# Linear attention: a head's decays, scores and states as three steps, tied behind the projections of a written order

## The chip, the cores and the metric

The kernel runs on one core of a Trainium2 chip. The metric is the device time of one execution in microseconds (us); lower is better. The core has a matrix engine (TensorE; PE in the profile, and PEld for its weight loads), a vector engine (VectorE, DVE), an activation engine (ScalarE, ACT), GpSimd (POOL) and SyncE (SP), which here mainly issues DMA transfers. Each engine takes its own instructions in the order in which they were put in its queue.

## The reference, cut to what matters

A diffusion-style block (token mixer with a gated delta rule and gated linear attention, then a mixture of 32 experts) is followed by two layers of a second block. The change lies in the gated linear attention (GLA) of the mixer: 4 heads, key size 128, value size 256, 256 context tokens and 256 latent tokens, each head scanned forwards and backwards.

```python
def gla_chunked(q, k, v, log_a, s0):          # S_t = diag(a_t) S_{t-1} + k_t v_t^T, o_t = S_t^T q_t
    gcum = jnp.cumsum(log_a, axis=-2)          # the decays, summed along a chunk
    ref = gcum[..., c // 2:c // 2 + 1, :]
    attn = einsum('bhnik,bhnjk->bhnij', q * exp(gcum - ref), k * exp(ref - gcum))   # scores
    intra = einsum('bhnij,bhnjv->bhniv', where(incl, attn, 0.0), v)
    qg, kd, gl = q * exp(gcum), k * exp(gcum[..., -1:, :] - gcum), exp(gcum[..., -1, :])
    def step(s, xs_n):
        o_n = intra_n + einsum('bhck,bhkv->bhcv', qg_n, s)
        s = s * gl_n[..., :, None] + einsum('bhck,bhcv->bhkv', kd_n, v_n)           # states
```

Around it stand the input projections (1024 inputs, more than 9000 columns), SiLU and sigmoid gates of them, an RMS norm of each head's output, and the output projections.

## The kernel before, in words

Everything here is in `phase1`, which ends before the experts begin. The projections are matrix products in a split precision: `load_w` (L172) brings 512 KB of weights from HBM through a ring of three buffers on SP's queue, `parts` splits them into a high part `wh` on ACT (L150) and a rest `wl` on DVE (L151), each in a pool of two buffers, and `mm3` (L164) makes three matmuls for each product, those with `wh` first and those with `wl` last. `proj_fm` uses one such load (24 matmuls of 256 columns for the latent tokens), `proj_tm` two loads (48 matmuls for two token tiles, 96 for four).

Tiles share buffers by tag. In PSUM there are two buffers of tag `mm` and two of `sm`, three of `ch` and one of `pu`. A planner in the framework (its scheduler) puts the instructions into the queues of the engines. It gets them in the order in which the program names them, keeps every dependence on data and buffers, and may put a later named instruction of an engine ahead of an earlier one if by its own model of times the earlier one would still be waiting.

The stage in question comes after the delta rule and is driven by the string `GLA_ORDER`, one letter for one piece of work:

- `D`, a head's gates, both directions. `gla_gates(h, d)` does one direction from end to end. First the decays: a small product into `ch` (L807, PE), the log-sigmoid `z`, `l` (L810 to L814, DVE and ACT), running sums `G` (L818, DVE), and from these on ACT and DVE the scaled queries and keys `qk` (L828 to L835), `off` (L837 to L841), `qs` (L842 to L844), `glt` (L846) and `kd` (L848 to L852). Then the scores: `kd` is transposed on PE (L855) and copied to `kdt` by ACT (L857); PE makes the scores (L862, L863), and DVE copies them under a mask into `AT` (L864). Then the states: PE (L868) into `pu`, ACT copies (L869), PE again (L871), DVE (L872) into `gs`. It returns `qs`, `AT` and `gs`.
- `O`, `outputs(h)`: the products of a head's `qs` with `gs` and of `AT` with the values `gv`, for both directions (L947, L948, PE), in buffers of tag `mm`.
- `v`: values of heads 2 and 3 (`proj_tm`, four tiles, all buffers of `mm` and `sm`); there are two `gv` buffers, so head 2's takes the place of head 0's.
- `S`: RMS of two delta heads, a quarter of the gate `z` (`silu_cols`, `proj_tm`), and `columns`, which multiplies, transposes on PE (L924) and splits (L929, L930). `R`: the same projection for the GLA branch. `B`: RMS and `columns` of one GLA head. `G` and `b`: one of eight sigmoid gates each (`gate_cols`, `proj_fm`).

The string before is `DSGGGGOvDSGODGSORvDSRGRBBBGbORbbBbbbbb`. Nothing in this stage but data, buffers and the planner's model sets where a piece stands in PE's queue. After the stage come the output projections (`w_out_a`, `w_out_b`), and on SP's queue the first weights of the experts.

Of the kernel before, what the change touches and what calls it, by code (L numbers as in the profile page):

```python
# [9 lines left out]
F32 = mybir.dt.float32  # L10
F32R = mybir.dt.float32r
# [176 lines left out]
DELTA_ORDER = "EkPPKPKPKPKMmXXXXXXXXXPQPQPVVHHkqSSSSSSSSPPQPQPVVHHSSSSSSSSEkPPKPKPKPKMXXXXXXXXXPQPQPVmVHHSSSSSSSSkPPQPQPVqqVHHSSSSSSSSqvv"  # L188


GLA_ORDER = "DSGGGGOvDSGODGSORvDSRGRBBBGbORbbBbbbbb"


def phase1(k, A, B):
# [25 lines left out]
    def smps(cols=512):  # L220
        return ps.tile([128, 512], F32, name=k.nm("sm"), tag="sm", bufs=2)[:, :cols]
# [8 lines left out]
    def big(shape, dt=F32):  # L230

        return y8.tile([128] + shape, dt, name=k.nm("y8"), tag="y8")
# [93 lines left out]
    for kk in range(8):  # L326
# [5 lines left out]
                                    op0=ALU.mult, op1=ALU.add)  # L332
        nc.vector.tensor_sub(hTl[:, kk, :], hf, hTh[:, kk, :].bitcast(F32))

    def at(x, i):
        return x[i] if isinstance(x, Halves) else x[:, i, :]

    def proj_fm(src, xh, xl):

        wh, wl = parts(k, load_w(k, src))  # L340
        o = mmps(xh.shape[-1])
        mm3(nc, o, [(wh[:, kk, :], wl[:, kk, :], at(xh, kk), at(xl, kk), True) for kk in range(8)], True, True)
        return o

    def proj_tm(src, tiles, xh, xl, evac):

        os_ = [None] * len(tiles)
        for half in range(2):
            wh, wl = parts(k, load_w(k, src[512 * half:512 * half + 512, :]))
            for i, t in enumerate(tiles):  # L350
                if half == 0:
                    os_[i] = ps.tile([128, 256], F32, name=k.nm("tm"), tag=("mm", "sm")[i // 2], bufs=2)
                ts = slice(t * 128, (t + 1) * 128)
                mm3(nc, os_[i], [(wh[:, kk, :], wl[:, kk, :], at(xh, 4 * half + kk)[:, ts], at(xl, 4 * half + kk)[:, ts], False)
                                 for kk in range(4)], half == 0, half == 1)
        for i, t in enumerate(tiles):
            evac(t, os_[i])

# [443 lines left out]
    def gla_gates(h, d):  # L802

        f = d == 0
        kT, qT = gk[h], gq[h]
        pz = ps.tile([128, 512], F32, name=k.nm("ch"), tag="ch", bufs=3)
        nc.tensor.matmul(pz, gw[32 * d:32 * d + 16, h * 128:(h + 1) * 128], lr[32 * d:32 * d + 16, :], start=True, stop=True)  # L807
        T2 = lambda nm, tag, b=2: (wd if tag == "kt" else wk).tile([128, 512], F32, name=k.nm(nm), tag=tag, bufs=b)
        z, l = T2("z", "acc"), T2("l", "e", 3)
        nc.vector.tensor_scalar_add(z, pz, vecT[:, 24 + 4 * d + h:25 + 4 * d + h])  # L810
        nc.scalar.activation(l, z, AF.Abs)
        nc.scalar.activation(l, l, AF.Exp, scale=-1.0)
        nc.scalar.activation(l, l, AF.Ln, bias=1.0)
        nc.vector.scalar_tensor_tensor(z, z, 0.0, l, op0=ALU.min, op1=ALU.subtract)  # L814
        G = T2("G", "kt")
        for c0, c1 in ((0, 256), (256, 384), (384, 512)):
            st = 1 if f else -1
            nc.vector.tensor_tensor_scan(G[:, c0:c1][:, ::st], one1.to_broadcast([128, c1 - c0]), z[:, c0:c1][:, ::st],  # L818
                                         0.0, op0=ALU.mult, op1=ALU.add)
        g2 = G[:, 256:512].rearrange("p (t c) -> p t c", c=128)  # L820
        g4 = G[:, 256:512].rearrange("p (t c) -> p t c", c=64)
        fh, sh = (slice(0, 64), slice(64, 128)) if f else (slice(64, 128), slice(0, 64))
        bnd = g2[:, :, 63:64] if f else g2[:, :, 64:65]
        fi = 0 if f else 1
        tc_, tl = (G[:, 255:256], G[:, 383:384]) if f else (G[:, 0:1], G[:, 384:385])
        x = wd.tile([128, 256], F32, name=k.nm("x"), tag="qT", bufs=4)
        x4 = x.rearrange("p (t c) -> p t c", c=64)
        nc.vector.tensor_tensor(x4, g4, g4[:, :, (32 if f else 31):(33 if f else 32)].to_broadcast([128, 4, 64]),  # L828
                                op=ALU.subtract)
        qk = wd.tile([128, 512], F32, name=k.nm("qk"), tag="kT", bufs=5)  # L830
        qe, ke = qk[:, 0:256], qk[:, 256:512]
        nc.scalar.activation(qe, x, AF.Exp, scale=0.0625)
        nc.scalar.activation(ke, x, AF.Exp, scale=-0.0625)
        nc.vector.tensor_mul(qe, qe, qT)
        nc.vector.tensor_mul(ke, ke, kT[:, 256:512])  # L835
        off = wd.tile([128, 2, 2, 64], F32, name=k.nm("off"), tag="qT", bufs=4)
        nc.vector.tensor_tensor(off[:, 0], g2[:, :, sh], bnd.to_broadcast([128, 2, 64]), op=ALU.subtract)  # L837
        nc.vector.tensor_tensor(off[:, 1], bnd.to_broadcast([128, 2, 64]), g2[:, :, fh], op=ALU.subtract)
        nc.scalar.activation(off, off, AF.Exp, scale=0.0625)
        nc.vector.tensor_mul(off[:, 0], off[:, 0], qT.rearrange("p (t c) -> p t c", c=128)[:, :, sh])  # L840
        nc.vector.tensor_mul(off[:, 1], off[:, 1], kT[:, 256:512].rearrange("p (t c) -> p t c", c=128)[:, :, fh])  # L841
        qs = wd.tile([128, 256], F32, name=k.nm("qs"), tag="os", bufs=2)  # L842
        nc.scalar.activation(qs, G[:, 256:512], AF.Exp, scale=0.0625)
        nc.vector.tensor_mul(qs, qs, qT)  # L844
        glt = wd.tile([128, 1], F32, name=k.nm("glt"), tag="glt", bufs=2)
        nc.scalar.activation(glt, tl, AF.Exp, scale=0.0625)  # L846
        kd = wd.tile([128, 384], F32, name=k.nm("kd"), tag="pad", bufs=2)
        nc.vector.tensor_tensor(kd[:, 0:256], tc_.to_broadcast([128, 256]), G[:, 0:256], op=ALU.subtract)  # L848
        nc.vector.tensor_tensor(kd[:, 256:384], tl.to_broadcast([128, 128]), g2[:, fi, :], op=ALU.subtract)
        nc.scalar.activation(kd, kd, AF.Exp, scale=0.0625)  # L850
        nc.vector.tensor_mul(kd[:, 0:256], kd[:, 0:256], kT[:, 0:256])
        nc.vector.tensor_mul(kd[:, 256:384], kd[:, 256:384], kT[:, 256 + fi * 128:384 + fi * 128])  # L852
        pk = smps(384)
        for t in range(3):
            nc.tensor.transpose(pk[:, t * 128:(t + 1) * 128], kd[:, t * 128:(t + 1) * 128], ident)  # L855
        kdt = wd.tile([128, 3, 128], F32, name=k.nm("kdt"), tag="A2", bufs=2)
        nc.scalar.copy(kdt.rearrange("p t c -> p (t c)"), pk)  # L857
        AT = wd.tile([128, 2, 128], F32, name=k.nm("AT"), tag="st", bufs=2)
        nc.gpsimd.memset(AT, 0.0)
        for t in range(2):  # L860
            pa = chps()
            nc.tensor.matmul(pa, ke[:, t * 128:(t + 1) * 128], qe[:, t * 128:(t + 1) * 128], start=True, stop=True)  # L862
            nc.tensor.matmul(pa[fh, sh], off[:, 1, t, :], off[:, 0, t, :], start=True, stop=True)  # L863
            nc.vector.copy_predicated(AT[:, t, :], m_gla[:, 128 * d:128 * d + 128], pa)  # L864
        ss_ = wd.tile([128, 2, 256], F32, name=k.nm("gs"), tag="vb", bufs=2)
        p0 = ps.tile([128, 256], F32, name=k.nm("pu"), tag="pu", bufs=1)
        for t in range(2):
            nc.tensor.matmul(p0, kdt[:, t, :], gv[h][:, t, :], start=(t == 0), stop=(t == 1))  # L868
        nc.scalar.copy(ss_[:, 0, :], p0)  # L869
        p1 = ps.tile([128, 256], F32, name=k.nm("pu"), tag="pu", bufs=1)  # L870
        nc.tensor.matmul(p1, kdt[:, 2, :], gv[h][:, 2 + fi, :], start=True, stop=True)  # L871
        nc.vector.scalar_tensor_tensor(ss_[:, 1, :], ss_[:, 0, :], glt, p1, op0=ALU.mult, op1=ALU.add)  # L872
        return qs, AT, ss_

    def silu_cols(c0, dst, ccs=range(4)):

# [64 lines left out]
    def outputs(h):  # L941
        for t in range(2):
# [5 lines left out]
                nc.tensor.matmul(po, AT[:, t, :], gv[h][:, 2 + t, :], start=False, stop=(d == 1))  # L948
            nc.scalar.copy(ob[:, t, h, :], po)

    for c in GLA_ORDER:
        i = count.setdefault(c, 0)
        count[c] += 1
        if c == "D":
            two[i] = [gla_gates(i, d) for d in range(2)]
        elif c == "O":
            outputs(i)
        elif c == "S":
            ba_.rms(2 * i, 2)
            silu_cols(3072, z, (i,))  # L960
            ba_.columns(i)
        elif c == "G":
            gate_cols(7232, ga, (i,))
        elif c == "v":
            fill_gv(i + 2)
        elif c == "R":
            silu_cols(6176, rr2, (i,))
        elif c == "B":
            if not bb:
                bb = [Branch(ob, 4, rr2, 33, big([8, 256], F32R), big([8, 256], F32R))]  # L970
            bb[0].rms(i, 1)
            bb[0].columns(i)
        else:
            gate_cols(8256, gb_, (i,))
    bb = bb[0]
# [1127 lines left out]
```

## Time and profile before

| | us |
|---|---|
| three runs | 2461.91, 2469.0, 2471.72 |
| median | 2469.0 |
| the profiled execution, its own time | 2463.59 |
| its span, first to last instruction | 2461.8 |

In the page's busy time PE has 2277.9 us (93% of the span), PEld 1546.1 (63%), DVE 1244.0 (51%), ACT 925.4 (38%), POOL 150.9 (6%). The mean granted clock of TensorE is 0.969 of full speed. HBM was read at 245 GB/s over the span. The 40 slices of the page are 61.5 us each: the GLA stage runs from the end of slice 8 to the middle of slice 11, and the experts' weights stream in slices 14 to 27. Times of views count from the start of the span. A PE row's busy time overlaps its neighbours', since a matmul starts before the one ahead of it has drained.

### The profile page before, as it was taken

How to read it: one execution, taken by the hardware profiler on the slowest of the kernel's cores; microseconds unless marked ns; L12 is line 12 of the kernel's file. 1: busy time of each engine (PE TensorE's matmuls, PEld its weight loads, DVE VectorE, ACT ScalarE, POOL GpSimd, SP SyncE). 2: the span in 40 equal slices, each digit the busy share in tenths (PEclk: the TensorE clock that was granted, in tenths of full speed). 3: DMA queues.
4: the chain of work that ended last, by engine and by line, in shares of the span. 5: the costliest groups of instructions: out<-in, count | busy, mean ns of one | idle time of the engine just before them, and what ended most of it. 6: DMA issues, size and time to landing. Idle time of an engine off the chain costs nothing.

```text
span 2461.8 us, 36281 instructions
## 1 busy us (share of the span) xinstructions
PE 2277.9 (93%) x14402; PEld 1546.1 (63%) x14403; DVE 1244.0 (51%) x2676; ACT 925.4 (38%) x1956; POOL 150.9 (6%) x186
## 2 busy tenths in 40 slices
PE   6789878999989999999899999998999999999998
PEld 3466556889983433333334333334877999887998
DVE  4898887587561111112211111114867556867655
ACT  4556546577441101010101010103475545465545
POOL 0122122000010000000000000000011001011001
PEclk8889988999999999999999999999999999999999
DMA  8522431134897999999999999996525555534563
GB/s 288 141 79 57 121 116 35 47 92 122 260 333 307 419 420 419 420 419 420 391 419 419 421 418 420 419 420 232 149 79 156 183 172 159 155 98 141 188 188 104
DMA packets 273963, 605.87 MB, mean 246 GB/s; under 512 B 26038, under 2 KB 218681, under 8 KB 221564
## 3 DMA queue, kind: packets, MB, share of 16 engines
q1 hardware_dynamic: 266852, 595.24, 65.7%
q10 hardware_dynamic: 6280, 7.80, 1.2%
q8 instruction: 115, 1.88, 0.3%
q14 instruction: 60, 0.49, 0.1%
q0 software_dynamic: 656, 0.46, 0.1%
HBM read 602.30 MB, written 1.15 MB: 245 GB/s over the span
## 4 chain that ended last, share of the span: by engine, by line
PE 34%; DMA 10%; DVE 4%; issue 2%; ACT 1%; POOL 0%; ACTq 0%; SPq 0%; DVEq 0%; POOLq 0%
PE qm L164 23%; DMA w<-in_w_gu_dram 7%; PE yd L1376 2%; DMA w<-in_w_down_dram 2%; PE gt L1360 2%; PE lt L1360 1%; PE qm L1814 1%; DVE wl L151 1%; PE tr L1345 1%; DVE u L1620 0%; DVE ul L151 0%; PE tr L1289 0%; PE qp L1881 0%; ACT wh L150 0%; PE lt L1365 0%
## 5 line engine op out<-in xcount | busy, mean ns | idle before, releaser
L150 ACT CAST wh<-w 128x1024 fp32r<-128x1024 f32 (+2 forms) x318 | 318.5, 1002 | 285.4 <-PE qm L164 203.6
L151 DVE TENSOR_TENSOR wl<-w,wh 128x1024 fp32r<-128x1024 f32 (+2 forms) x318 | 371.4, 1169 | 39.9 <-ACT wh L150 38.2
L1253 ACT ACTIVATE sg<-g 128x1024 f32<-128x1024 f32 x16 | 16.9, 1057 | 720.4 <-DVE g L1251 720.4
L164 PE MATMUL qm<-uh,wh 128*128 128x272 f32 (+2 forms) x1008 | 261.8, 294 | 0.5 <-ACT wh L150 0.3
L164 PE MATMUL qm<-ul,wh 128*128 128x272 f32 (+2 forms) x1008 | 258.4, 289 | 1.2 <-DVE ul L151 1.2
L1251 DVE TENSOR_SCALAR g<-gt 128x1024 f32<-128x1024 f32 x16 | 19.6, 1225 | 462.9 <-PE gt L1365 407.3
L1376 PE MATMUL yd<-w,aT 128*64 128x512 f32 x1024 | 228.6, 601 | 0.0
L164 PEld LDWEIGHTS qm<-uh,wh 128*128 128x128 f32 (+1 forms) x1008 | 189.2, 188 | 10.2 <-issue 5.8
L164 PEld LDWEIGHTS qm<-ul,wh 128*128 128x128 f32 (+1 forms) x1008 | 189.9, 189 | 3.1 <-DVE ul L151 1.6
L1360 PE MATMUL lt<-w,resB 128*64 128x512 f32 x512 | 187.9, 593 | 0.6 <-DVE act L1252 0.6
L1360 PE MATMUL gt<-w,resB 128*64 128x512 f32 x512 | 183.0, 600 | 4.8 <-DMA w<-in_w_gu_dram 4.8
L1360 PE MATMUL lt<-w,xg 128*64 128x512 f32 x512 | 185.3, 593 | 0.0
L1360 PE MATMUL gt<-w,xg 128*64 128x512 f32 x512 | 175.3, 597 | 8.6 <-DMA w<-in_w_gu_dram 8.5
L1376 PEld LDWEIGHTS yd<-w,aT 128*64 128x64 f32 x1024 | 73.0, 139 | 142.6 <-issue 139.8
L1275 DVE TENSOR_TENSOR ys<-yd,g2r 128x512 f32<-128x512 f32 x32 | 20.6, 686 | 249.5 <-PE yd L1376 233.0
L164 PE MATMUL qm<-uh,wl 128*128 128x272 f32 (+2 forms) x1008 | 145.4, 286 | 0.0
L164 PE MATMUL mm<-hTh,wh 128*128 128x256 f32 (+1 forms) x384 | 130.1, 358 | 8.5 <-ACT wh L150 4.1
L164 PEld LDWEIGHTS qm<-uh,wl 128*128 128x128 f32 (+1 forms) x1008 | 132.6, 188 | 0.5 <-issue 0.4
L164 PE MATMUL qm<-fl,wh 128*128 128x272 f32 (+1 forms) x512 | 128.5, 286 | 0.0
L164 PE MATMUL qm<-fh,wh 128*128 128x272 f32 (+1 forms) x512 | 127.3, 286 | 0.0
L164 PE MATMUL mm<-hTl,wh 128*128 128x256 f32 (+1 forms) x384 | 125.9, 347 | 0.0
L1360 PEld LDWEIGHTS lt<-w,resB 128*64 128x64 f32 x512 | 57.7, 137 | 74.1 <-issue 72.1
(586 smaller groups left out, 4349.3 us busy)
## 6 DMA issues: line engine op xcount, KB each, us to landing
w<-in_w_gu_dram SPq DMA_DIRECT2D x256, 1024.0 KB
w<-in_w_down_dram SPq DMA_DIRECT2D x128, 1024.0 KB
w<-in_w_ff_dram SPq DMA_DIRECT2D x64, 1024.0 KB
w<-in_w_in_dram SPq DMA_DIRECT2D x72, 512.0 KB
w<-in_w_in_dram SPq DMA_DIRECT2D x30, 1024.0 KB
y<-in_w_mod_dram SPq DMA_DIRECT2D x19, 1024.0 KB
w<-in_w_out_dram SPq DMA_DIRECT2D x24, 512.0 KB
w<-in_w_mod_dram SPq DMA_DIRECT2D x5, 1024.0 KB
```

The lines of the kernel that those rows point to most:

```text
L150: k.nc.scalar.copy(hi, x)
L151: k.nc.vector.tensor_sub(lo, x, hi.bitcast(F32))
L164: mm = nc.tensor.matmul(out, l, r, start=start and n == 1, stop=stop and n == 3 * len(terms))
L1251: nc.vector.tensor_scalar(g, gt, 7.0, LOW / 1.702, op0=ALU.min, op1=ALU.max)
L1253: nc.scalar.activation(sg, g, AF.Exp, scale=-1.702)
L1275: nc.vector.tensor_mul(ys[:, js], yd[:, js], g2r[:, js])
L1345: nc.tensor.matmul(o, hx[:, t, f * 128:(f + 1) * 128], S[t].rearrange("p e s -> p (e s)"), start=(t == 0 and i == 0), stop=(t == 1 and i = ...
L1360: nc.tensor.matmul(quarter(j)[64 * i:64 * i + 64], xg[:, kk, c0:c0 + CAP], w[i][:, j * 512:(j + 1) * 512], start=(kk == 0), stop=False)
L1376: nc.tensor.matmul(yd[64 * i:64 * i + 64, j * 512:(j + 1) * 512], aT[:, 2 * f2 + f, 64 * i:64 * i + 64], w[i][:, f, j * 512:(j + 1) * 512] ...
L1814: nc.tensor.matmul(o[r, f:], v[:n, j, r], keys(ts[i], j, n)[:, f - KQ[j]:], start=(j == 0), stop=(j == 2))
```

## The change

The string becomes a longer one of 62 letters. `D` is gone: `gla_gates` is now a generator that stops twice, and each direction of each head is three letters, `d` (decays, up to `kd`), `e` (transposes and scores) and `f` (states). `S` is split too: `s` does the RMS and the projection, `C` does `columns`. The letters `d`, `e`, `f`, `O`, `C` and `B` run under `tc.issue_after(made_by[0].ins)`, where `made_by[0]` is the last matmul of the projection named last: every PE instruction of such a letter must stand behind that matmul in PE's queue. The instructions of other engines get no such edge, and a projection may still be put ahead. `qs` takes a buffer of tag `kT` (five of them) and no longer one of the two of tag `os`. No instruction is added or removed.

```diff
-GLA_ORDER = "DSGGGGOvDSGODGSORvDSRGRBBBGbORbbBbbbbb"
+
+GLA_ORDER = "dsdGCefdGGGGefOdvefdsGCefOdvefdsGCefOdRsefGCRBefORBBbRbbBbbbbb"
...
+    made_by = [None]
+
...
-        mm3(nc, o, [(wh[:, kk, :], wl[:, kk, :], at(xh, kk), at(xl, kk), True) for kk in range(8)], True, True)
+        made_by[0] = mm3(nc, o, [(wh[:, kk, :], wl[:, kk, :], at(xh, kk), at(xl, kk), True) for kk in range(8)], True, True)
...
-                mm3(nc, os_[i], [(wh[:, kk, :], wl[:, kk, :], at(xh, 4 * half + kk)[:, ts], at(xl, 4 * half + kk)[:, ts], False)
-                                 for kk in range(4)], half == 0, half == 1)
+                made_by[0] = mm3(nc, os_[i], [(wh[:, kk, :], wl[:, kk, :], at(xh, 4 * half + kk)[:, ts],
+                                               at(xl, 4 * half + kk)[:, ts], False) for kk in range(4)], half == 0, half == 1)
...
-        qs = wd.tile([128, 256], F32, name=k.nm("qs"), tag="os", bufs=2)
+        qs = wd.tile([128, 256], F32, name=k.nm("qs"), tag="kT", bufs=5)
...
         nc.vector.tensor_mul(kd[:, 256:384], kd[:, 256:384], kT[:, 256 + fi * 128:384 + fi * 128])
+        yield
         pk = smps(384)
...
             nc.vector.copy_predicated(AT[:, t, :], m_gla[:, 128 * d:128 * d + 128], pa)
+        yield
         ss_ = wd.tile([128, 2, 256], F32, name=k.nm("gs"), tag="vb", bufs=2)
...
-        return qs, AT, ss_
+        yield qs, AT, ss_
...
+    def pinned(c, i):
+        if c in "def":
+            h, d = divmod(i, 2)
+            if c == "d":
+                two.setdefault(h, []).append(gla_gates(h, d))
+                next(two[h][d])
+            else:
+                x = next(two[h][d])
+                if c == "f":
+                    two[h][d] = x
+        elif c == "O":
+            outputs(i)
+        elif c == "C":
+            ba_.columns(i)
+        else:
+            if not bb:
+                bb.append(Branch(ob, 4, rr2, 33, big([8, 256], F32R), big([8, 256], F32R)))
+            bb[0].rms(i, 1)
+            bb[0].columns(i)
+
     for c in GLA_ORDER:
         i = count.setdefault(c, 0)
         count[c] += 1
-        if c == "D":
-            two[i] = [gla_gates(i, d) for d in range(2)]
-        elif c == "O":
-            outputs(i)
-        elif c == "S":
+        if c in "defOCB":
+            with tc.issue_after(made_by[0].ins):
+                pinned(c, i)
+        elif c == "s":
             ba_.rms(2 * i, 2)
             silu_cols(3072, z, (i,))
-            ba_.columns(i)
...
-        elif c == "B":
-            if not bb:
-                bb = [Branch(ob, 4, rr2, 33, big([8, 256], F32R), big([8, 256], F32R))]
-            bb[0].rms(i, 1)
-            bb[0].columns(i)
```

With heads and directions written out, the new string begins d(0,0) s0 d(0,1) G0 C0 e(0,0) f(0,0) d(1,0) G1 G2 G3 G4 e(0,1) f(0,1) O0 d(1,1) v2 e(1,0) f(1,0) d(2,0) s1 G5 C1 e(1,1) f(1,1) O1 d(2,1) v3, and goes on e(2,0) f(2,0) d(3,0) s2 G6 C2 e(2,1) f(2,1) O2 d(3,1) R0 s3 e(3,0) f(3,0) G7 C3 R1 B0 e(3,1) f(3,1) O3 R2 B1 B2 b R3 b b B3 and five more b.

## Rows read from the trace of the kernel before

**Rows 1.** The page's 40 slices: busy tenths, granted clock, transfer rate.

```profile
PE   6789878999989999999899999998999999999998
...
PEclk8889988999999999999999999999999999999999
...
GB/s 288 141 79 57 121 116 35 47 92 122 260 333 307 419 420 419 420 419 420 391 419 419 421 418 420 419 420 232 149 79 156 183 172 159 155 98 141 188 188 104
```

**Rows 2.** Stretches: PE, PEld, DVE, ACT, POOL busy (instructions), clock, DMA share, GB/s.

```profile
474.00:641.90 167.90, 164.96 (x1205) 149.88 (x1204) 131.52 (x320) 120.99 (x300) 1.87 (x6) 1.00 0.43 119
641.90:650.00 8.10, 5.75 (x36) 5.55 (x35) 3.71 (x5) 5.64 (x10) 2.34 (x1) 0.79 0.69 205
```

**Rows 3.** Waits of PE's matmuls, 474.5 to 646: total us, times, longest.

```profile
PE ch L862 <- DVE qk L835: 2.8, 6, 0.6
PE mm L164 <- ACT wh L150: 2.4, 1, 2.4
```

**Rows 4.** Groups of PEld, 474.5 to 642: busy, mean ns | idle before, releasers.

```profile
L164 PEld LDWEIGHTS tm<-wh,hTh 128*128 128x128 f32 x189 | 35.7, 189 | 1.1 <-issue 0.8
...
L862 PEld LDWEIGHTS ch<-qk 128*128 128x128 f32 x32 | 4.3, 190 | 4.0 <-PE tm L164 2.5 <-PE mm L164 0.8 <-DVE qk L835 0.6
L924 PEld LDWEIGHTS sm<-cst,yt 128*128 128x128 f32 x32 | 3.9, 140 | 1.4 <-issue 0.5 <-PE mm L164 0.3 <-DVE yt L919 0.2
...
L871 PEld LDWEIGHTS pu<-gv,kdt 128*128 128x128 f32 x16 | 2.4, 188 | 0.9 <-ACT gs L869 0.8
```

**Rows 5.** Timeline of PE around one of those waits: start, us, what.

```profile
483.81 0.28 PE L164 MATMUL mm<-hTl,wh 128*128 128x256 f32 x1
483.93 0.28 PE L164 MATMUL mm<-hTh,wh 128*128 128x256 f32 x1
484.60 0.71 PE L862 MATMUL ch<-qk 128*128 128x128 f32 x4 [0.39 <-DVE qk L835]
...
485.62 1.12 PE L807 MATMUL ch<-lr,gw 16*128 16x512 f32 x2
486.67 0.39 PE L164 MATMUL mm<-hTl,wh 128*128 128x256 f32 x1
```

**Rows 6.** Groups of DVE, 474 to 642, columns as in the fourth group.

```profile
L151 DVE TENSOR_TENSOR wl<-w,wh 128x1024 fp32r<-128x1024 f32 x35 | 42.5, 1220 | 15.7 <-ACT wh L150 15.7
L818 DVE TENSOR_TENSOR_SCAN G<-ones,z 128x128 f32<-128x128 f32 (+1 forms) x24 | 10.6, 495 | 0.1
...
L810 DVE TENSOR_SCALAR z<-ch,vecT 128x512 f32<-128x512 f32 x8 | 6.0, 748 | 0.7 <-PE ch L807 0.6
L814 DVE SCALAR_TENSOR_TENSOR z<-z,l 128x512 f32<-128x512 f32 x8 | 5.5, 688 | 1.9 <-ACT l L813 1.9
...
L828 DVE TENSOR_TENSOR x<-G 128x256 f32<-128x256 f32 x8 | 3.3, 416 | 0.0
...
L852 DVE TENSOR_TENSOR kd<-kd,resA 128x128 f32<-128x128 f32 x8 | 2.3, 285 | 0.0
```

**Rows 7.** Stretches of head 0, and of the value projection after it.

```profile
474.50:505.20 30.70, 29.73 (x203) 25.83 (x203) 27.72 (x68) 25.05 (x61) 0.31 (x1) 1.00 0.37 104
505.20:516.10 10.90, 10.90 (x92) 10.85 (x92) 6.23 (x21) 5.17 (x14) 0.31 (x1) 1.00 0.38 98
```

**Rows 8.** Timeline from the transposes of head 0, direction 1, to its output.

```profile
498.69 0.49 PE L855 MATMUL sm<-cst,kd 128*128 128x128 f32 x3
...
499.89 1.03 PE L868 MATMUL pu<-gv,kdt 128*128 128x256 f32 x4
...
501.39 0.70 PE L871 MATMUL pu<-gv,kdt 128*128 128x256 f32 x2
...
502.87 0.59 PE L947 MATMUL mm<-gs,qs 128*128 128x256 f32 x2
```

**Rows 9.** Timelines of SP and ACT at the end of the stage.

```profile
630.63 0.37 SPq L1007 DMA_DIRECT2D resA<-in_x_dram  x1
...
643.44 1.04 ACT L150 CAST wh<-w 128x1024 fp32r<-128x1024 f32 x1 [4.68 <-DMA w<-in_w_out_a_dram]
```

## The prediction

> **What bounds the kernel now.** I read the strip of 40 slices first. In the stage that the change touches (slices 8 to 11) PE shows 9 or 8 tenths and the clock 9, so PE is the engine in question there; in slices 14 to 27 transfers run at about 419 GB/s, and that stretch is bound by the experts' weights, which the change doesn't touch [rows 1]. The stage can only shift it.
>
> Second I read the stage as a stretch, from the first gates at 474.0 to the last projection at 641.9 us: 167.9 us, PE busy 164.96, DVE 131.52, ACT 120.99, clock 1.00, that is 2.4 GHz throughout [rows 2]. By this PE is idle for 167.9 - 164.96 = 2.9 us, and no order of the same instructions can win much more than that inside the stage. The stretch behind it, 641.9 to 650, has PE busy for 5.75 of 8.1 us at a mean clock of 0.79.
>
> Third, who ends PE's idle time: six waits of the scores for `qk`, 2.8 us together, and one wait of 2.4 us for the cast of the first `w_out_a` weights [rows 3]. The list for the weight loads, which come first of each pair, puts 4.0 us before the scores, 0.9 before the second state product and 1.4 before the transposes of `columns` [rows 4]. The timeline shows one such place: the projection's matmuls start every 0.12 us (483.81, 483.93), and the last of these is followed by the scores only at 484.60, and the projection goes on behind them [rows 5]. Nothing that the projection needs is late; it stands behind the scores in the queue. So the planner believed that `qk` would be ready about half a microsecond before it was.
>
> **The change, part by part.**
>
> *The edge behind the projection named last.* Scores and states are held back until a projection is through, and in the new string the decays `d` are named one step earlier than `e`. Only e(0,0) follows its `d` closely: s0 and G0 lie between, 72 matmuls at the 0.12 us spacing of [rows 5], 8.6 us, against the 10 us that passed from the gate product at 474.5 (where the stretch of head 0 begins) to the scores at 484.60 [rows 5, 7]. Behind d(0,1) lie G0 to G4 (120 matmuls, 14 us), behind d(1,0) the whole of G1 to G4 and v2, and so on: every other `e` has 10 us and more. The wait before the scores therefore should go at five of six places: 4.0 x 5/6 = 3.3 us by the loads' list, 2.8 x 5/6 = 2.3 us by the matmuls' list. Of the 0.9 + 1.4 = 2.3 us before the state product and `columns` [rows 4] I take half, 1.1 us, because `C` now has an edge of its own behind a gate projection while `e` and `f` still follow each other directly. Gain 3.3 + 1.1 = 4.4 us; lower bound 2.3, upper bound all of it, 4.0 + 2.3 = 6.3 us.
>
> *Steps put together.* `e`, `f` and `O` now stand in a row. Their chain runs from the transposes at 498.69 to the product with the new state at 502.87, 4.2 us, of which PE works 0.49 + 1.03 + 0.70 = 2.2 us itself; the other 2.0 us are copies on ACT and DVE, and today matmuls of projections fill them [rows 8]. The planner may still fill them. It lacks filler most where `v` follows `O`: the value projection wants both `mm` buffers, which `O` uses, so only its two tiles in `sm` can start, and the half of `O` that needs direction 0 alone. I count 0.4 us for it; bounds nothing and 2.0 us at each of eight places.
>
> *DVE.* The new string asks for one direction more before O0, d(1,0), and for a fifth gate projection. A `d` costs DVE, summed over eight: 10.6 + 6.0 + 5.5, six groups like L828's 3.3 (its own, both of `qk`, `qs`, two of `kd`) and six like L852's 2.3 (two of `kd`, four of `off`), 55.7 us, so 7.0 us each [rows 6]. In head 0's stretch DVE is busy for 27.72 of 30.70 us [rows 7]. With 7.0 us for d(1,0) and, for the fifth gate, 1.2 for the split of its weights (L151) and 0.4 for a maximum as large as L828's tile [rows 6] that becomes 36.3; PE's work becomes 29.73 + 24 x 0.12 + 1.1 for L807, 33.7 [rows 5, 7]. DVE would be short by 2.6 us if all of d(1,0) had to be done before O0. It need not: its scores come behind v2, where DVE is busy for 6.23 of 10.90 us [rows 7]. I take nothing here, covered by v2; if that cover is gone it costs 2.6 us once.
>
> *The `kT` buffer for `qs`, `made_by`, the two stops of the generator.* They issue nothing. Two of the five `kT` buffers per direction hold `qk` and `qs`, so the third direction's `qs` takes the buffer that e(0,0) frees, which is named before. Nothing.
>
> *Queues.* No transfer is added; the 512 KB loads follow the projections' new order on SP, with DMA at 0.43 of its time in the stage [rows 2]. On ACT the exponentials of the next direction now stand ahead of some casts; `glt` and `kd` have two buffers each, so they wait for the state and transposes of two directions earlier, and casts queue behind them. This is inside the 0.4 us above.
>
> *The end of the stage.* The string ends as before, R3 b b B and five b. The load of `x` goes out at 630.63, when the last `columns` has read its buffer, ahead of the first `w_out_a` weights, which ACT gets only at 643.44 after 4.68 us of waiting [rows 9]. I take it as unchanged. If `columns` comes earlier against the projections, at most PE's 2.4 us go [rows 3] and with them the slow clock: (1 - 0.79) x 8.1 = 1.7 us [rows 2]; if later, as much is lost. Bounds -4 to +4 us.
>
> Sum: -4.4 + 0.4 = -4.0 us on 2463.6, so 2459.6 for an execution like the profiled one. That one lies 5.4 us under the median of 2469.0; against the median the same gain gives **2465.0 us**. A measurement of this kernel can tell about 0.5%, 12.3 us, from no change, and the whole idle time of PE in the stage is less than that.
>
> **A measure that speaks for more.** By the loads, PE's share looks different: PEld is idle for 167.9 - 149.88 = 18.0 us of the stage [rows 2]. But 0.8 us of it stand behind each L807, where the next load waits while PE is at its 1.12 us product [rows 4, 5], and such time is no room; I find 6.3 us of real waits. The Trainium skill (Perfetto Trace Analysis, "Identifying the Most-Contended Engine") says that matmul busy time flatters the engine and that the busy share of the weight loads is to be used instead. By that page all 18.0 us would be room, and the sum could reach 2451. The trace agrees only in part: the loads' list holds more waits than the matmuls' list, 4.0 against 2.8 before the scores.
>
> **The rivals.**
>
> *It does nothing that can be seen.* The planner already places scores where it believes them ready, and its error of half a microsecond reappears before the transposes of `kd`, which come first in `e`. For: L855 now needs `kd`, made after `qk`. Against: five of six have 10 us and more of slack. Time 2463 to 2469 against the median.
>
> *Slower: bare chains.* PE runs `e`, `f` and `O` with nothing in between, since the next projection finds no free `mm` buffer or its weights aren't split. Each bare chain costs 2.0 us [rows 8]; two of eight eat up the gain, all eight cost 16 us: -4 + 16 = +12, 2481. For: all three letters wait for the same matmul. Against: only matmuls behind the edge are held, projections may come ahead, as they do in the stretch of [rows 5]. Four bare: +4, 2473.
>
> *Faster: the loads' idle time was room.* 18 us, 2451; against it the row of L807. *The end of the stage moves*, -4 or +4 us on top: 2461 or 2469.
>
> **How the numbers follow.** Forecast (gain of 1.5 to 6 us) 0.52; nothing to be seen 0.26; bare chains 0.12, of which 0.07 over 12.3 us, the planner's other changes of order included; the loads' room 0.05; the end moving, 0.05. The first, second and last are all within 0.5%, as is part of the third: faster by over 0.5% 0.06 (the loads' room and a little of the last), same 0.86, slower 0.08. The likeliest case alone holds 2463 to 2467.5. The range must take in the end moving with the gain (2461), four to six bare chains (2473 to 2477), and that the three runs shown lie from 7 under to 3 over their median: 2454 to 2477.
>
> **What the new profile would show.** Right: PE's waits of L862 down from six to one or two, under 1 us; the stretch from the first L807 to the last matmul before `w_out_a` shorter by 3 to 5 us, with DVE, ACT and instruction counts as before; L855 ahead of L862 in every `e`. Wrong: idle time before L868, L871 or L947 that adds to more than 2 us (bare chains); waits of `wl` casts before a projection in head 0 (DVE short); a wait for the first `w_out_a` weights well over 4.7 us (the end of the stage); or a stage that is shorter than PE's 165 us of work, by which the busy time would have held room after all.

## The result, and the profile after

The changed kernel takes 2487.19 us (median of four runs, 2484.71 to 2489.96); the kernel before, on the same chip, 2469.2 us (2461.91 to 2471.72). The ratio is 1.0076, 95% interval 1.0062 to 1.0091: slower by 18 to 19 us, outside the predicted range of 2454 to 2477. The profiled execution has a span of 2486.2 us.

The stage comes first: the page's strips of PE and the clock after the change, which answer to [rows 1].

```profile
PE   6789979988898999989899999998999999999998
...
PEclk8789988999998999999999999999999999999999
```

The loss can't be placed in it: slices 9 to 11 now show 8 on PE where [rows 1] had 9; other slices differ by as much either way. So I take the stage as one stretch, from the first gate product (477.9) to the last projection matmul (664.6), and six stretches of 10 us inside it; columns as in [rows 2].

```profile
477.90:664.60 186.70, 171.14 (x1203) 153.67 (x1202) 131.90 (x320) 121.41 (x297) 1.87 (x6) 0.97 0.37 108
490.00:500.00 10.00, 7.52 (x52) 6.28 (x50) 9.93 (x28) 9.20 (x26) 0.00 (x0) 1.00 0.20 52
500.00:510.00 10.00, 6.32 (x39) 5.92 (x40) 9.91 (x25) 5.71 (x15) 0.00 (x0) 0.83 0.19 54
540.00:550.00 10.00, 8.33 (x59) 7.24 (x58) 9.53 (x26) 8.79 (x27) 0.11 (x1) 1.00 0.35 107
570.00:580.00 10.00, 8.33 (x70) 8.13 (x70) 9.12 (x23) 7.90 (x17) 0.00 (x0) 1.00 0.07 15
590.00:600.00 10.00, 8.01 (x58) 7.83 (x58) 8.21 (x21) 6.52 (x17) 0.00 (x0) 0.88 0.32 91
620.00:630.00 10.00, 7.71 (x38) 6.44 (x39) 2.98 (x9) 2.95 (x8) 0.00 (x0) 0.83 0.13 47
```

With the same bounds the stage of before is 167.7 us long with PE busy for 164.74. So it grew by 19.0 us, as much as the kernel did. (The two profiled spans differ by 24.4: ahead of the stage, where the engines' queues are the same in both, this execution is 3.4 us later, and behind it 2.0 us longer; the first gate product of the fourteen profiles of this document lies anywhere between 474.0 and 483.3, so this is no effect of the change.) The instructions are the same (1203 matmul records, DVE 320), but PE is idle for 186.7 - 171.14 = 15.6 us in place of 3.0, and its busy time rose by 6.4 us at a mean clock of 0.97 in place of 1.00. In the first four of the short stretches DVE is busy for 9.1 to 9.9 of 10 us while PE is busy for 6.3 to 8.3; in the fifth both are at 8, and in the last one DVE is hardly busy.

The chain is not needed to see who ends PE's idle time; the waits of the stage name it (columns as in [rows 3]):

```profile
PE mm L164 <- DVE y L894: 4.1, 1, 4.1
PE sm L929 <- DVE yt L924: 3.4, 3, 3.0
PE mm L164 <- DVE zx L886: 3.3, 2, 1.7
PE mm L164 <- DVE wl L151: 2.1, 1, 2.1
PE tm L164 <- DVE zx L886: 2.0, 1, 2.0
PE pu L876 <- ACT gs L874: 0.5, 1, 0.5
PE mm L164 <- DVE rst L133: 0.2, 1, 0.2
```

The six waits of the scores for `qk` [rows 3], the only sort that before has in this stage, are gone, as forecast. All that stands here is new. Lines are three to five higher now, so L894 and L886 are the DVE instructions that read a finished projection out of PSUM, L151 the split of its weights: in 4.1 + 3.3 + 2.1 + 2.0 = 11.5 of 15.6 us *projections* wait for DVE. The other large one is the transposes of `columns` (L929), 3.4 us.

### The profile page after: what moved, and what is told of

Same layout as the page of the kernel before. It is cut to its first block, busy times and chain, and to the rows that moved or that the text cites. A ratio compares the mean times of both kernels' runs of the same rounds, so it can differ in the third digit from the quotient of the medians.

```text
span 2486.2 us, 36274 instructions
## 1 busy us (share of the span) xinstructions
PE 2291.9 (92%) x14402; PEld 1556.5 (63%) x14403; DVE 1245.9 (50%) x2676; ACT 926.8 (37%) x1956; POOL 150.8 (6%) x186
## 5 line engine op out<-in xcount | busy, mean ns | idle before, releaser
L151 DVE TENSOR_TENSOR wl<-w,wh 128x1024 fp32r<-128x1024 f32 (+2 forms) x318 | 372.2, 1171 | 46.7 <-ACT wh L150 44.5
```

What stands on the lines that cost most here:

```text
L151: k.nc.vector.tensor_sub(lo, x, hi.bitcast(F32))
```

## The experiments

Three suspicions: the new order itself (more decays, `d`, named early, DVE crowded); the edges (scores held behind a projection that is itself late); and the buffer of `qs`. Each run below gives its ratio to the kernel before on the same chip with its 95% interval, and the length of the stage in its profile, measured from first gate product to last projection matmul; before it is 167.7 us, changed 186.7.

**1. The edges away, order and buffer kept.**

```diff
-            with tc.issue_after(made_by[0].ins):
-                pinned(c, i)
+            pinned(c, i)
```

> The changed kernel with its new string, but the letters d, e, f, O, C and B run without the edge behind the last named projection. Theory A (the gate chains of the new string come closer together on DVE, and the reads that free the projections' mm buffers and the splits of weights queue behind them): the edges are not the cause, the time stays at 2482 to 2490 us, and PE still waits for the maxima of the projections. Theory B (the edges hold scores, states and outputs back until their copies lie bare): about 2469 us, like before.

1.0030 (1.0012 to 1.0047), 2472.23 us, stage 177.3 us: between the two theories and nearer B. More than half of the loss goes with the edges (0.46 of 0.76%), so neither the order nor the edges alone is the whole. Of the 11.5 us for which projections waited for these four, 0.2 us is left, and a wait of the scores has come back:

```profile
PE ch L866 <- DVE qk L838: 1.5, 1, 1.5
...
PE tm L164 <- DVE zx L886: 0.2, 1, 0.2
```

The two profiles show what an edge does. In the changed kernel, PE from 497.2 and DVE from 490.3:

```profile
497.25 0.28 PE L164 MATMUL mm<-hTl,wh 128*128 128x256 f32 x1
501.60 0.36 PE L164 MATMUL mm<-hTh,wh 128*128 128x256 f32 x1 [4.08 <-DVE y L894]
...
502.45 0.41 PE L164 MATMUL mm<-hTl,wh 128*128 128x256 f32 x1
502.66 0.41 PE L164 MATMUL mm<-hTh,wh 128*128 128x256 f32 x1
...
507.08 2.33 PE L164 MATMUL mm<-hTh,wl 128*128 128x256 f32 x16 [2.08 <-DVE wl L151]
...
618.24 0.59 PE L953 MATMUL mm<-gv,AT 128*128 128x256 f32 x2
621.83 0.48 PE L929 MATMUL sm<-cst,yt 128*128 128x128 f32 x1 [2.99 <-DVE yt L924]
```

```profile
490.35 0.41 DVE L894 TENSOR_SCALAR y<-mm 128x256 f32<-128x256 f32 x1
...
499.84 0.28 DVE L855 TENSOR_TENSOR kd<-kd,resA 128x128 f32<-128x128 f32 x1
...
500.44 0.68 DVE L817 SCALAR_TENSOR_TENSOR z<-z,l 128x512 f32<-128x512 f32 x1
501.04 0.41 DVE L894 TENSOR_SCALAR y<-mm 128x256 f32<-128x256 f32 x1
501.37 1.31 DVE L821 TENSOR_TENSOR_SCAN G<-ones,z 128x256 f32<-128x256 f32 x3
...
505.61 0.28 DVE L855 TENSOR_TENSOR kd<-kd,resA 128x128 f32<-128x128 f32 x1
505.81 2.35 DVE L151 TENSOR_TENSOR wl<-w,wh 128x1024 fp32r<-128x1024 f32 x2
...
618.28 0.75 DVE L888 TENSOR_TENSOR rr<-zx,rr 128x256 f32<-128x256 f32 x2
```

By the order of the string, the matmul at 497.25 is the last with `wh` of G2; then none starts for 4.3 us. G3, which is next, needs the `mm` buffer of G1, and the reading of that (L894 at 501.04) stands in DVE's queue behind all of d(0,1), which ends with L855 at 499.84, and the first of d(1,0). When it has come, G3's matmuls with `wh` run; those with `wl`, eight of G2 and eight of G3, wait until 507.08, since the two splits stand behind the rest of d(1,0), which ends with L855 at 505.61. The same without edges, on PE:

```profile
494.67 0.28 PE L164 MATMUL mm<-hTl,wh 128*128 128x256 f32 x1
496.42 0.68 PE L866 MATMUL ch<-qk 128*128 128x128 f32 x4 [1.48 <-DVE qk L838]
497.03 0.45 PE L867 MATMUL ch<-off 128*64 128x64 f32 x4
497.41 1.12 PE L810 MATMUL ch<-lr,gw 16*128 16x512 f32 x2
498.46 0.63 PE L859 MATMUL sm<-cst,kd 128*128 128x128 f32 x3
499.66 1.22 PE L873 MATMUL pu<-gv,kdt 128*128 128x256 f32 x2 [0.57 <-ACT kdt L861]
500.32 0.78 PE L164 MATMUL mm<-hTh,wh 128*128 128x256 f32 x1
```

and on DVE:

```profile
498.46 0.42 DVE L894 TENSOR_SCALAR y<-mm 128x256 f32<-128x256 f32 x1
...
503.23 2.35 DVE L151 TENSOR_TENSOR wl<-w,wh 128x1024 fp32r<-128x1024 f32 x2
```

DVE does the same in both: counted from the first gate product (477.9 and 475.3), L894 comes at 23.1 and 23.2 us, the split at 27.9 and 27.9. DVE is no less behind without the edges; but PE, free to leave the stuck projection, does the scores, a gate product, the transposes and the first state product of e and f(0,1) in that time. With the edge these stand behind G4, the projection named last, and so behind the stuck one. The same rows carry the clock: in the changed kernel matmuls follow at 0.21 us after the pause (502.45, 502.66), where 0.12 is the full clock's spacing [rows 5]; this is the lower of the clock's two levels, 1.2 GHz.

**2. The old order in the new letters, with edges.**

```diff
-GLA_ORDER = "dsdGCefdGGGGefOdvefdsGCefOdvefdsGCefOdRsefGCRBefORBBbRbbBbbbbb"
+GLA_ORDER = "defdefsCGGGGOvdefdefsCGOdefdefGsCORvdefdefsCRGRBBBGbORbbBbbbbb"
```

> The changed kernel with the old order written in the new letters (D as d e f d e f, S as s C), edges and the kT buffer for qs kept. Theory A: the gates of a direction are named behind the scores of the one before, so the chains are as far apart as before, 10 us and more; 2465 to 2473 us. Theory B: the edges still hold PE's steps back, 2480 us or more.

1.0064 (1.0042 to 1.0085), stage 185.6 us. So the edges (with the buffer) cost nearly as much in the old order. Its waits are mostly of another kind, though: PE is idle for 185.6 - 173.0 = 12.6 us, and in 7.2 of them scores wait for `qk`. Run 5 says how much of it was the buffer.

**3. The decays in pairs**, so that DVE gets a head's two directions together and later.

```diff
-GLA_ORDER = "dsdGCefdGGGGefOdvefdsGCefOdvefdsGCefOdRsefGCRBefORBBbRbbBbbbbb"
+GLA_ORDER = "dsdGCefGGGGefOddvefsGCefOddvefsGCefOddRsefGCRBefORBBbRbbBbbbbb"
```

> The changed kernel with d(h+1,0) named behind O(h) beside d(h+1,1), and no longer behind the first states of head h: both directions' gates lie under the value projection (or R0 and s3), as the D of the old string did. Theory A: head 0 gets back its 4.3 and 2.6 us waits and their slow clock, some of the later ones move; 2470 to 2479 us. Theory B: no change, 2484 to 2490 us.

1.0088 (1.0054 to 1.0122), 2486.87 us, stage 185.4 us. No better, as theory B had it: the waits for `zx` and `y` are 7.5 and 3.4 us, the same kind of wait in other places. That it is the early d(1,0) alone fell here.

**4. DVE relieved:** five products of each `d` go to GpSimd.

```diff
-        nc.vector.tensor_mul(off[:, 0], off[:, 0], qT...)
+        nc.gpsimd.tensor_mul(off[:, 0], off[:, 0], qT...)
...
-        nc.vector.tensor_mul(qs, qs, qT)
+        nc.gpsimd.tensor_mul(qs, qs, qT)
...
```

(and likewise the other half of `off` and both halves of `kd`)

> The changed kernel with five multiplications of each d (off twice, qs, kd twice; 0.28 + 0.28 + 0.41 + 0.41 + 0.28 = 1.7 of 7.0 us on DVE) on GpSimd, which is idle. Theory A: DVE's queue gets shorter by 1.7 us at each of eight chains, and PE's waits with it: 2475 to 2482 us, unless GpSimd takes so long that scores and states wait for it. Theory B: 2484 to 2490 us.

1.0051 (1.0030 to 1.0071), 2479.11 us, stage 183.8 us. The time lies where theory A had it, but the intervals of this run and of the change overlap, so a gain is not shown by the times. In the profiles PE's idle time is 183.8 - 172.75 = 11.0 us in place of 15.6, while its busy time rose by 1.6. The groups of GpSimd in the stage show its products, and two groups of DVE what they do there.

```profile
L854 POOL TENSOR_TENSOR kd<-kd,resA 128x256 f32<-128x256 f32 x8 | 10.0, 1249 | 0.0
...
L847 POOL TENSOR_TENSOR qs<-qs,gq 128x256 f32<-128x256 f32 x8 | 6.5, 807 | 0.0
...
L886 DVE TENSOR_SCALAR zx<-tm 128x256 f32<-128x256 f32 x16 | 6.7, 419 | 1.4 <-PE tm L164 1.4
...
L888 DVE TENSOR_TENSOR y<-zx,y 128x256 f32<-128x256 f32 x8 | 4.7, 595 | 0.0
```

The same groups in the changed kernel, all on DVE:

```profile
L886 DVE TENSOR_SCALAR zx<-tm 128x256 f32<-128x256 f32 x16 | 6.5, 418 | 1.9 <-PE tm L164 1.9
...
L854 DVE TENSOR_TENSOR kd<-kd,resA 128x256 f32<-128x256 f32 x8 | 3.3, 415 | 0.0
...
L888 DVE TENSOR_TENSOR y<-zx,y 128x256 f32<-128x256 f32 x8 | 3.2, 416 | 0.0
```

L854 takes 1249 ns in place of 415, and DVE's own L888 595 in place of 416, while L886, which reads PSUM, stays at 419. The splits (L151) took 1313 ns on average in place of 1220. So DVE's busy time in the stage fell only from 131.90 to 128.43 us, though eight times 1.7 us of work had left it.

**5. The buffer alone:** the kernel before, with `qs` in `kT`.

```diff
-        qs = wd.tile([128, 256], F32, name=k.nm("qs"), tag="os", bufs=2)
+        qs = wd.tile([128, 256], F32, name=k.nm("qs"), tag="kT", bufs=5)
```

> The kernel before with qs in the kT buffers and nothing else. It differs from e2 (old order, edges, kT) in the edges alone. Theory C (two costs: the new order, and the edge on e, which keeps scores, states and outputs from filling PE while DVE is behind): within 3 us of before, 2464 to 2470 us, so that all of e2's loss is the edges'. Rival K (the buffer lets gates run ahead and is the cause in e2): 2474 to 2481 us.

1.0036 (1.0021 to 1.0051), 2476.10 us, stage 177.1 us: an edit that I had costed at nothing. The time is that of rival K, the mechanism is not, for gates come later and not ahead. In this run's timeline of PE the gate product of head 1 stands behind the values, at 516.35, not within head 0's scores as before (497.10); the chains that follow are late, and the longest wait of scores is 3.6 us:

```profile
PE ch L862 <- DVE qk L835: 5.5, 6, 3.6
```

Against run 2, which has the same order and buffer and the edges too, the edges cost 1.0064 - 1.0036 = 0.28% in the old order, with an interval of about 0.26% either way, so this is barely clear of nothing.

**6 and 7. B0 later,** with edges and without. In the new string the first `columns` of the GLA branch are named between R1 and e(3,1).

```diff
-GLA_ORDER = "...RsefGCRBefORBBbRbbBbbbbb"
+GLA_ORDER = "...RsefGCRefORBBBbRbbBbbbbb"
```

> The changed kernel with the letter B0 named behind R2 beside B1 and B2, no longer between R1 and e(3,1): its transposes, which wait for yt, no longer stand ahead of e(3,1) and O3. Theory C: the waits of 3.4 and 1.0 us at 618 and 624 go, and some of the slow clock behind them; 2480 to 2484 us. Rival: the chain of e(3,1), f(3,1) and O3 stays bare and the wait only moves to it: 2485 to 2489 us.

> The changed kernel without the edges (as e1) and with B0 named behind R2 (as e6). Theory C: of e1's loss against before the 3.4 and 1.3 us at its end go: 2466 to 2469 us, level with before. Rival: as e1, 2471 to 2473 us.

With edges 1.0046 (1.0026 to 1.0066), 2477.46 us, stage 181.7 us; without 0.9997 (0.9983 to 1.0012), 2465.17 us, stage 170.1. Both gained a little more than theory C said. The 3.4 us wait of L929 falls to 0.2 in both. In the timelines of the changed kernel above, at the end: DVE's last product for R1 is at 618.28, the RMS of B0 follows it on ACT and DVE, and PE stands at B0's transposes from 618.83, when the product of 618.24 ends, to 621.83, with e(3,1) and f(3,1) queued behind them.

**8. The relief of run 4 in the kernel before.**

```diff
-        nc.vector.tensor_mul(qs, qs, qT)
+        nc.gpsimd.tensor_mul(qs, qs, qT)
```

(and the other four, as in run 4)

> The kernel before with five multiplications of each direction's gates (1.7 of 7.0 us) on GpSimd. If DVE is what the stage's last idle time hangs on: the six waits for qk shrink, 2461 to 2466 us. If GpSimd takes as much longer as DVE saves, the scores of head 0 wait for off and kd: 2467 to 2475 us.

1.0159 (1.0135 to 1.0184), 2505.90 us, stage 209.3 us: far above both ranges. Where scores follow their decays at once, slower products stand in the chain: the transposes of `kd` now wait for GpSimd 4.4 us (L851) and 1.0 us (L852), the second scores 3.5 us. So the products on GpSimd are no relief as such. In run 4 whole projections lie between decays and scores, and PE waits for GpSimd 0.2 us.

**9 to 12. The buffer undone in the new string,** which makes all eight cases of edges, buffer and place of B0.

```diff
-        qs = wd.tile([128, 256], F32, name=k.nm("qs"), tag="kT", bufs=5)
+        qs = wd.tile([128, 256], F32, name=k.nm("qs"), tag="os", bufs=2)
```

(and with it the edits of runs 1 and 6: 9 neither, 10 no edges, 11 late B0, 12 both)

> The changed kernel with one edit undone: qs has its old two buffers of tag os again; string and edges stay. Theory (the loss is a sum of separate parts, and the buffer is one of them, +0.36% in the old order): about 9 us less than the changed kernel, 2478 (ratio 1.004), stage (first gate product to last projection matmul) near 178 us. Rival (the buffer cost something only in the old order, where it moved the third gate chain behind the values projection; in the new string the letters place that chain): 2485 to 2488, ratio 1.0070 to 1.0080, stage 185 to 188.

> The new string alone: old qs buffers, no edges. If the buffer is a part of its own: 1.0030 - 0.0036, about 1.000, stage 169 us. Rival (the buffer is harmless in the new string): as with the kT buffer and no edges, 1.003, stage 177. Either way the 3.4 us wait of PE for the first columns of the GLA branch should be there, since B0 stands where the change put it.

> Old qs buffers and B0 moved behind R2, edges kept: what remains of the change is the new string and the edges. Sum of parts: 1.0076 - 0.0036 - 0.0030 = 1.001, stage about 173 us. Rival (buffer harmless in the new string): 1.0046, stage 182, as with the kT buffer. If the edges are the largest single part, the run stays above 1.003 in either case only under the rival.

> New string with B0 behind R2, old qs buffers, no edges: the candidate. Sum of parts: 0.9997 - 0.0036 = 0.996, 2457 us; but the stage would then be 161 us, less than the 165 us that PE is busy in it, so the sum can't hold whole: about 166 us of stage and 0.998 at best. Rival: 0.9997 again, stage 170.

All eight, ratio with half-width of its interval, and length of the stage less PE's busy time in it:

| new string with | `qs` in `kT` | `qs` in `os` |
|---|---|---|
| edges, B0 early | 1.0076 ±0.0015; 186.7 - 171.1 = 15.6 (the change) | 1.0058 ±0.0015; 182.7 - 169.4 = 13.3 (9) |
| edges, B0 late | 1.0046 ±0.0020; 181.7 - 169.6 = 12.1 (6) | 1.0037 ±0.0013; 178.8 - 169.2 = 9.6 (11) |
| no edges, B0 early | 1.0030 ±0.0018; 177.3 - 170.6 = 6.7 (1) | 1.0039 ±0.0014; 176.9 - 171.5 = 5.4 (10) |
| no edges, B0 late | 0.9997 ±0.0015; 170.1 - 166.7 = 3.4 (7) | 0.9999 ±0.0012; 170.9 - 168.8 = 2.1 (12) |

Down the columns, the edges cost 0.46, 0.49, 0.19 and 0.38%, on average 0.38% or 9.4 us of 2467; the early B0 costs 0.30, 0.33, 0.21 and 0.40%, on average 0.31% or 7.7 us. Each of these differences has an interval of about 0.2% either way, the average of four, taken as independent, about 0.1%; by the stages, one profile each, the averages are 8.7 and 5.5 us. Across, the buffer costs 0.18, 0.09, -0.09 and -0.02%: 0.04% on average, nothing that these intervals tell from zero. My theory before these four, that the buffer is a part of the loss like the other two, fell: runs 10 and 12 came out as the rival said, 9 and 11 between the two, and a cost of the buffer is shown in the old order only (run 5).

The last row is the new string without edges and with B0 late. The waits of run 12's stage, and its stage as a stretch with two shorter ones:

```profile
PE sm L859 <- DVE kd L854: 0.6, 1, 0.6
PE pu L873 <- ACT kdt L861: 0.6, 1, 0.6
PE pu L876 <- ACT gs L874: 0.5, 1, 0.5
PE sm L929 <- DVE yt L924: 0.2, 1, 0.2
```

```profile
480.00:650.90 170.90, 168.79 (x1207) 153.22 (x1206) 131.67 (x325) 121.84 (x303) 1.87 (x6) 0.98 0.41 116
490.00:500.00 10.00, 9.71 (x67) 8.02 (x65) 9.83 (x33) 8.90 (x28) 0.00 (x0) 1.00 0.00 0
500.00:510.00 10.00, 9.07 (x37) 7.40 (x38) 7.95 (x16) 6.51 (x14) 0.00 (x0) 0.66 0.51 137
```

Not one wait of scores is left, and PE's idle time is 2.1 us, less than before; but the stage is 3.2 us longer, since its busy time is 168.79 and not 164.74, at a clock of 0.98 and not 1.00, and the kernel's time is the same. No version beats the kernel before.

## Why the prediction was wrong

*What bounds the kernel.* Nothing here speaks against it: the 3 us of PE's idle time in the stage were named as the most that an order could win, and no run's stage is shorter than 167.7 us. (Slices 8 to 11 show 9 on PE in all four [rows 1], not 9 or 8; nothing hangs on it.) But it was read for gains alone. A stage with PE busy for 98% of it and DVE for 78% has little to win and, if PE is made to wait for DVE, much to lose; that belonged in the chances.

*The waits of the scores, -3.3 us.* Right as to the mechanism: 2.8 us and six of them before, none after. The gain didn't stay, even without edges: in run 12 other short waits have come, one of them 0.6 us before the transposes of `kd`, the place that the rival "it does nothing that can be seen" named. The order with B0 late is worth 0.9997 to 0.9999, so that rival was right about such a string, and -4.4 us were too much; as it stood in the change, without edges, the string cost 0.30 and 0.39% (runs 1 and 10).

*The edge.* This is the step that failed. I counted it as a gain, with 0.4 us against it for steps put together. It costs 9.4 us on average of four pairs. The prediction's price went by the copies inside `e` and `f` (2.0 us a place, the rival "bare chains"), and it asked whether projections could fill the holes between scores. It is the reverse: scores, gate products and transposes had filled the holes of the projections, and 11.5 of the 15.6 us of PE's idle time are projections that wait for DVE. L876 waits 0.5 us once, so bare chains they are not, though that rival's 2481 came nearest; that was its size and not its mechanism.

*DVE, "nothing, covered by v2".* The other half of the same failure. The shortage was seen (2.6 us in head 0) and then excused, because the scores of d(1,0) are not needed before v2. But it isn't the scores that suffer: DVE takes its queue in order, d(1,0) stands ahead of the reading of G1, whose buffer G3 needs, and of the splits for G2 and G3, and two waits of 4.1 and 2.1 us follow. It isn't d(1,0) alone, since run 3 named it later and the waits only moved. The sign that I had named, a wait for `wl` in head 0, came with 2.1 us. Two stretches of 10 us of the profile of before (columns as in [rows 2]) show the danger:

```profile
480.00:490.00 10.00, 9.61 (x71) 8.35 (x69) 9.73 (x29) 9.10 (x26) 0.00 (x0) 1.00 0.20 53
490.00:500.00 10.00, 9.42 (x68) 8.05 (x67) 9.75 (x25) 8.01 (x21) 0.00 (x0) 1.00 0.37 107
```

DVE is busy there for 9.73 and 9.75 us, and the new string names one more `d` into just these. The thing to price was what stands behind the seven microseconds of a `d` in DVE's queue, not only who needs its result.

*The `kT` buffer, "nothing".* In the new string no cost is shown, 0.04% ± some 0.1; but not for the reason given, since in the old order the same edit moves a gate chain by 19 us and costs 0.36%. That no buffer runs short doesn't say that the planner places things as before.

*The end of the stage, "as before", bounds ±4 us.* Failed: I read only the last letters, R3 b b B. Eight letters ahead of that R3 the first B had come to stand between R1 and e(3,1), and costs 7.7 us on average of four pairs, more than the bound: in the profiles of runs 1 and 7, 6.7 - 3.4 = 3.3 us of idle time and 170.6 - 166.7 = 3.9 of PE's busy time at the lower clock. The wait for the first `w_out_a` weights itself hardly moved: ACT waits 5.45 us for them, after 4.68 [rows 9].

*Queues and loads.* Right: DMA share 0.37 of the stage, no wait of PE for a load in it, and one of ACT, 0.3 us.

*The measure by the loads' idle time,* 18 us of room, found no support. PEld is idle for 170.9 - 153.22 = 17.7 us in run 12, where PE is idle for 2.1. The Trainium skill (Perfetto Trace Analysis, "Identifying the Most-Contended Engine") wants TensorE's headroom judged by the busy share of the weight loads, and beside it by the arithmetic done as a share of the peak, and calls matmul busy time no good measure; that it errs on the flattering side is the prediction's reading. Here no run turned any of the 18 us into a shorter stage.

*The sum.* Edges 9.4 + B0 7.7 us + the string and buffer at about nothing = 17 us against 18 to 19 measured. By the profile, the 19.0 us of the stage are 12.6 us more of idle time and 6.4 us more of busy time for the same matmuls, at a clock of 0.97. Inside the stage the prediction had no term for this second part; it counted a slower clock only behind it.

What stays open: that the edges cost only 0.19% in one of the four pairs (runs 9 and 10) is within the intervals' reach; in its profiles run 10 has 7.9 us less of idle time than run 9 but 2.1 us more of busy time, at a clock of 0.96 in place of 0.99. The edges of the six letters were only taken away together, so which of them costs how much is not shown. By what reckoning the planner moves the gate chain of head 1 in run 5 is open too; the timelines show only that it does.

## What to carry to other kernels

Before tying work behind something, ask what that work had been filling: here scores were PE's stopgap while a projection waited for DVE, and the edge took it away, for 9 us lost where at most 3 were to be won. A chain that is named earlier is priced by what then stands behind it in each engine's queue, not by who needs its result. And in a string of pieces compare the place of every letter with the old one; one piece named too early, with a long chain of its own (B0), cost 7.7 us beside the 9.4 of all the edges.

## What the runs showed of the hardware

A pause of PE can be paid twice, once as idle time and again as a slower clock behind it, but not each is. After the 4.3 us pause at 497 the matmuls ran at 0.21 us spacing, 1.2 GHz, and the stretch 500 to 510 has a mean clock of 0.83; the two stretches from 540 and 570 with 1.67 us of idle time each keep 1.00. Yet in run 12 the stretch 500 to 510 shows 0.66 with PE busy for 9.07 of 10 us. From 498.73 on PE had done scores, transposes and state products there, in pieces with two waits of 0.6 us; the gate products behind them already took 1.45 us where the pair took 1.12 before [rows 5]:

```profile
502.50 1.45 PE L810 MATMUL ch<-lr,gw 16*128 16x512 f32 x2
```

So the clock fell where no wait of PE was longer than 0.65 us, and the length of a pause alone doesn't foretell it.

GpSimd's product of 128x256 took 0.81 to 1.25 us on average where DVE's took 0.42 (times on GpSimd are rough in these profiles). Beside it some of DVE's products of two SBUF inputs became slower and those that read PSUM did not. Of the eight L888 of the group above, three ran wholly beside a product of GpSimd and took 0.79 to 0.95 us, the other five beside none and 0.41 to 0.42; of the sixteen L886, six ran beside one and kept 0.41 to 0.42. Not every one with two SBUF inputs pays: of eleven splits (L151) that ran beside a product of GpSimd, six took 1.74 to 1.78 us and five 1.21 to 1.22, as alone. The Trainium skill (SBUF — State Buffer, "Who interferes with whom") says that a DVE instruction with two SBUF inputs contends with a GpSimd instruction that reads SBUF; L888 and L886 agree with it, and so do six of the eleven splits.
